# A triangular solver given to one engine and cut into parts, products tied to block sums, and separate load buffers for one engine's weights

## The chip, the core and the metric

The kernel runs on one core of a Trainium2 chip. Five engines work side by side, each through a fixed list of instructions: TensorE (PE, matrix products; PEld is its weight load), VectorE (DVE), ScalarE (ACT), GpSimd (POOL) and SyncE (SP), which issues nearly all transfers. An instruction waits until the results that it needs are there, and everything behind it on the same engine waits too. The metric is the time of one execution in device microseconds (us).

## The reference, cut to what matters

Two layers over 1024 tokens of width 1024, all in float32:

```python
h = rmsnorm(x, norm_w); proj = h @ w_in
attn = neighbourhood_attention(rmsnorm(aq), rmsnorm(ak), av, rpb) * silu(az)      # 8 heads of 64
# gated delta net, chunks of 64 tokens: a unit lower triangular system for each of 128 chunks
a_mat = where(strict, (kb @ k.T) * decay, 0) + eye(64)
sol = triangular_solve(a_mat, rhs, lower=True, unit_diagonal=True)
...
x1 = x + concat([attn, delta]) @ w_out
# second layer: rmsnorm, w_in_2 (8 heads of 128 with stick breaking, retention, merge logits), w_out_2
```

## The kernel before

**Matrix products.** A float32 operand is split into a high and a low part, and each product is made of three passes (hi·hi, hi·lo, lo·hi). The weights are loaded by rows of 128 (k = 0 to 7) into a tile called raw (L59 to 64, one SP transfer each) and split into wu. For most weights POOL makes both parts (L70 the high one, L71 the low one). With fast=True, used for w_out and for the eight heads of the second layer, the odd k go another way: ACT casts the high part (L67) and DVE subtracts (L68). All raw tiles come from one ring of three buffers, whoever splits them. dense_tok (L91) makes token tiles m of 128 in a PSUM bank of three ("acc").

**The solver.** X holds 128 systems, one per partition, of 64 rows by 64 columns, in SBUF. Column j from 62 down to 1 takes two instructions for each group of rows: multiply into a scratch tile (L457), add into X (L459). Rows from 8 up are DVE's (scratch svt, 512 elements), rows below 8 POOL's (scratch svq, 256), and the last eight columns DVE's. When all is done, X is stored to d_X, which the merges of the delta net read. The solver is a generator: take(sol, 4) emits four columns ahead of each of the 16 tiles of the neighbourhood attention na_attn, whose own work for a tile is two score products, a softmax (L554 to 557), transposes and the value products. take(prj, 1) emits a piece of the projection na_proj of the next pair of heads, with its normalisation of q and k (L490 to 500), beside it.

**The norm between the layers.** For half the tokens (s = 0) normalize(0) makes eight products (L911), each followed by a cast on ACT (h2h) and a subtraction (h2l, L913, even k on POOL, odd on DVE). They are emitted between the blocks of the other half of w_out, whose results residual() adds to the input (L860) and stores to d_x1. With s = 1 the same is done under the first head of the second layer.

**The order.** Nobody writes the engines' lists by hand: the code gives work in the order of its statements, and a scheduler with its own estimate of times makes a fixed list for every engine. So an edit in one place can move instructions of another.

## Time and profile before

| what | value |
|---|---|
| time, median of 3 executions | 2250.16 us (2249.15 to 2255.03) |
| time of the profiled execution | 2252.17 us |
| its span on the core | 2250.5 us |
| PE busy | 2163.0 us, 96% of the span |
| mean granted clock of PE | 0.984 |
| DVE, ACT, POOL busy | 1102.5, 766.0, 1105.4 us |

The span is what the profiler saw on the core; 1.67 us lie around it. PE is busy nearly all of the time, so time can be won only where PE stands still or runs at a lower clock. The stages with which the change has to do lie in the span as follows: the solver from 295 to 500 us, the norm between the layers from 786 to 840, the first head of the second layer from 837, the eight heads until 1370.

### The profile page before, as it was taken

The page shows a single profiled execution, that of the slowest core. Times are in us where ns is not written, and L with a number is a line of the kernel's source. Part 1 is how long each engine was busy: PE and PEld are TensorE (multiplying, and loading weights), DVE is VectorE, ACT ScalarE, POOL GpSimd, SP SyncE. Part 2 cuts the span into 40 slices and gives each one's busy share as a digit, 9 for nine tenths or more (in the row PEclk, how much of TensorE's full clock was granted, in tenths as well). Part 3 has the DMA queues.
Part 4 walks back from the last instruction along what each step waited for, and adds up shares of the span by engine and source line. Part 5 has one row for each costly group of instructions (what it writes and reads, how often), then busy time and mean ns, then how long its engine had stood idle before and what let it go on. Part 6 is the DMA issues. An engine that isn't in the chain of part 4 may idle for free.

```text
span 2250.5 us, 33410 instructions
## 1 busy us (share of the span) xinstructions
PE 2163.0 (96%) x12325; PEld 1882.8 (84%) x12325; DVE 1102.5 (49%) x1980; ACT 766.0 (34%) x1912; POOL 1105.4 (49%) x1451
## 2 busy tenths in 40 slices
PE   7999888899999999999999999999999999999999
PEld 7777777787889878999999998888988888878887
DVE  4688879953446553566555655123333432231321
ACT  5354433445555322444333433112222322321200
POOL 6667777773101345344333334356565755354532
PEclk9999999899999999999999999999999999999999
DMA  4255740126377542111111112212333323564433
GB/s 132 83 152 157 206 129 26 36 82 190 90 278 246 176 130 63 41 61 57 57 42 34 43 57 71 89 58 79 107 94 120 126 92 114 179 227 159 146 109 106
DMA packets 240196, 250.27 MB, mean 111 GB/s; under 512 B 40161, under 2 KB 175521, under 8 KB 239777
## 3 DMA queue, kind: packets, MB, share of 16 engines
q1 hardware_dynamic: 240032, 248.14, 35.3%
q8 instruction: 97, 1.59, 0.3%
q14 instruction: 67, 0.54, 0.1%
HBM read 172.56 MB, written 75.53 MB: 110 GB/s over the span
## 4 chain that ended last, share of the span: by engine, by line
PE 68%; DVE 11%; POOL 6%; issue 5%; DMA 5%; ACT 2%; SPq 1%; POOLq 0%; DVEq 0%; ACTq 0%
PE acc L112 29%; PE acc L102 17%; PE acc L853 3%; PE po L1083 2%; PE pz L1051 2%; DVE X L459 2%; DVE svt L457 2%; POOL wu L71 2%; DVE cv L314 1%; POOL wu L70 1%; DMA raw<-in_w_in_dram 1%; PE pz L546 1%; PE pt L563 1%; POOL ss L126 1%; PE pp L577 1%
## 5 line engine op out<-in xcount | busy, mean ns | idle before, releaser
L112 PE MATMUL acc<-h2h,wu 128*128 128x512 f32 x1440 | 438.4, 393 | 0.7 <-ACT lg L958 0.7
L102 PE MATMUL acc<-wu,h2h 128*128 128x384 f32 (+1 forms) x1536 | 366.8, 322 | 6.6 <-ACT lg L972 2.2
L71 POOL TENSOR_TENSOR wu<-raw,wu 128x512 fp32r<-128x512 f32 (+3 forms) x276 | 366.3, 1335 | 7.2
L70 POOL TENSOR_SCALAR wu<-raw 128x512 fp32r<-128x512 f32 (+3 forms) x276 | 205.8, 749 | 313.0 <-PE acc L112 202.4
L112 PEld LDWEIGHTS acc<-h2h,wu 128*128 128x128 f32 x1440 | 269.5, 188 | 54.9 <-ACT lg L958 1.1
L102 PEld LDWEIGHTS acc<-wu,h2h 128*128 128x128 f32 x1536 | 265.8, 191 | 11.6 <-ACT lg L972 2.6
L112 PE MATMUL acc<-h2l,wu 128*128 128x512 f32 x720 | 265.2, 392 | 0.0
L102 PE MATMUL acc<-wu,h2l 128*128 128x384 f32 (+1 forms) x768 | 244.9, 321 | 0.0
L102 PE MATMUL acc<-wu,h1hi 128*128 128x384 f32 (+2 forms) x768 | 192.2, 334 | 11.1 <-DVE kS L512 5.2
L112 PE MATMUL acc<-h1hi,wu 128*128 128x512 f32 x512 | 167.3, 416 | 6.8 <-ACT pad L309 3.2
L125 POOL TENSOR_SCALAR ss<-ss 128x2 f32<-128x2 f32 (+2 forms) x136 | 36.7, 270 | 269.6 <-ACT sq L1001 215.0
L112 PEld LDWEIGHTS acc<-h2l,wu 128*128 128x128 f32 x720 | 135.0, 188 | 26.5
L102 PEld LDWEIGHTS acc<-wu,h1hi 128*128 128x128 f32 x768 | 137.0, 195 | 16.0 <-issue 6.5
L102 PEld LDWEIGHTS acc<-wu,h2l 128*128 128x128 f32 x768 | 146.1, 191 | 1.6
L112 PEld LDWEIGHTS acc<-h1hi,wu 128*128 128x128 f32 x512 | 100.4, 198 | 31.8 <-ACT pad L309 4.2
L102 PE MATMUL acc<-wu,h1lo 128*128 128x384 f32 (+2 forms) x384 | 126.7, 333 | 0.0
L126 POOL TENSOR_TENSOR ss<-ss,mhalf 128x2 f32<-128x2 f32 (+2 forms) x136 | 118.9, 875 | 8.3
L112 PE MATMUL acc<-h1lo,wu 128*128 128x512 f32 x256 | 97.9, 411 | 0.0
L1001 ACT ACTIVATE sq<-acc 128x128 f32<-128x128 f32 x128 | 35.5, 286 | 138.7 <-PE acc L102 125.8
L314 DVE SCALAR_TENSOR_TENSOR cv<-pad,c_conv_w,cv 128x1024 f32<-128x1024 f32 x48 | 76.6, 1596 | 1.1
L112 PE MATMUL acc<-oah,wu 128*128 128x512 f32 x256 | 76.1, 393 | 1.0 <-DVE sg L1275 0.6
L102 PEld LDWEIGHTS acc<-wu,h1lo 128*128 128x128 f32 x384 | 74.8, 195 | 0.4 <-issue 0.2
(553 smaller groups left out, 4438.1 us busy)
## 6 DMA issues: line engine op xcount, KB each, us to landing
raw<-in_w_in_dram SPq DMA_DIRECT2D x192, 256.0 KB, 3.0
d_pk<-sct SPq DMA_DIRECT2D x24, 512.0 KB, 4.3
raw<-in_w_out_dram SPq DMA_DIRECT2D x40, 256.0 KB, 3.0
wsa<-d_pk SPq DMA_DIRECT2D x16, 512.0 KB, 6.4
wsb<-d_pk SPq DMA_DIRECT2D x16, 512.0 KB, 7.4
d_sg<-lg SPq DMA_DIRECT2D x32, 256.0 KB, 2.4
sg<-d_sg SPq DMA_DIRECT2D x32, 256.0 KB, 3.4
raw<-in_w_in_dram SPq DMA_DIRECT2D x32, 192.0 KB, 2.8
```

The source lines that it names most:

```text
L70: nc.gpsimd.tensor_scalar(out=u[:, 0, :], in0=raw, scalar1=1.0, scalar2=0.0, op0=ALU.mult, op1=ALU.add)
L71: nc.gpsimd.tensor_tensor(out=u[:, 1, :], in0=raw, in1=f32(u[:, 0, :]), op=ALU.subtract)
L102: nc.tensor.matmul(acc[:, :n], lhsT=hT[a][:, k, m * P:(m + 1) * P], rhs=us[k][:, b, c0:c0 + n], start=(k == 0 and i == 0), stop=(k == NK - ...
L112: nc.tensor.matmul(accs[half], lhsT=us[k][:, b, c0:c0 + P], rhs=hT[a][:, k, half * 512:(half + 1) * 512], start=(k == 0 and i == 0), stop= ...
L125: nc.gpsimd.tensor_scalar(out=dst, in0=src, scalar1=mul, scalar2=eps, op0=ALU.mult, op1=ALU.add)
L126: nc.gpsimd.tensor_tensor(out=dst, in0=dst, in1=mhalf[:, :eshape], op=ALU.pow)
L314: nc.vector.scalar_tensor_tensor(out=cv, in0=pad[:, i:i + T], scalar=conv_w[:, blk, i:i + 1], in1=cv, op0=ALU.mult, op1=ALU.add)
L457: eng.tensor_tensor(out=tv, in0=X[:, a:a + n, j:j + 1].to_broadcast([P, n, w]), in1=X[:, j:j + 1, j + 1:64].to_broadcast([P, n, w]), op=AL ...
L459: eng.tensor_tensor(out=X[:, a:a + n, j + 1:64], in0=X[:, a:a + n, j + 1:64], in1=tv, op=ALU.add)
L853: nc.tensor.matmul(acc, lhsT=us[k][:, y, (b % 4) * P:(b % 4 + 1) * P], rhs=token_set(mT[x][:, k, 0:T], s), start=(k == 0 and i == 0), stop ...
L1051: nc.tensor.matmul(pz[:, :w], lhsT=qk[0][a][:, i * P:(i + 1) * P], rhs=qk[1][b][:, c0:c0 + w], start=(x == 0), stop=(x == 2))
L1083: nc.tensor.matmul(po[:, i0 * P:512], lhsT=v[a][:, c0 // P + kb, :], rhs=wT[b][:, :n], start=(diag and kb == 0 and x == 0), stop=(diag == ...
```

## The change

It does five things. The solver has DVE alone, with one scratch tile of 512, is cut into 16 parts of about equal work, and each part is emitted behind a tile of na_attn instead of ahead of it. The products that normalise q and k read the PSUM bank themselves, where ACT copied q and k to SBUF first. The broadcast copy rb moves from DVE to ACT. Each product of the first norm (s = 0) is ordered behind the last residual sum emitted so far, and two are emitted after a block in place of one. And the raw tiles of odd k of the eight heads come from two buffers of their own (tag rawf), in the pool sr of the second layer.

```diff
-    def split_unit(src, ncol, pool=None, tag="wu", parts=1, fast=False, rpool=None):
-        raw = (rpool or wraw).tile([P, ncol], F32, tag="raw", name="raw", bufs=8 if rpool else 3)
+    def split_unit(src, ncol, pool=None, tag="wu", parts=1, fast=False, rpool=None, fpool=None):
+        if fast and fpool:
+            raw = fpool.tile([P, ncol], F32, tag="rawf", name="raw", bufs=2)
+        else:
+            raw = (rpool or wraw).tile([P, ncol], F32, tag="raw", name="raw", bufs=8 if rpool else 3)
...
-    def solver():
+    def solver(parts):
         tmp = svp.tile([P, 512], F32, name="svt")
-        tmq = svp.tile([P, 256], F32, name="svq")
-        LOW = 8
...
-        for j in range(62, 0, -1):
-            if j > LOW:
-                update(nc.vector, tmp, 512, LOW, j, j)
-            update(nc.gpsimd if j >= LOW else nc.vector, tmq, 256, 0, min(j, LOW), j)
-            yield 1
+            w = 63 - j
+            step = -(-j // -(-j * w // 512))
+            for a in range(0, j, step):
+                n = min(step, j - a)
+                tv = tmp[:, :n * w].rearrange("p (r c) -> p r c", r=n)
+                nc.vector.tensor_tensor(out=tv, in0=X[:, a:a + n, j:j + 1].to_broadcast([P, n, w]),
+                                        in1=X[:, j:j + 1, j + 1:64].to_broadcast([P, n, w]), op=ALU.mult)
+                nc.vector.tensor_tensor(out=X[:, a:a + n, j + 1:64], in0=X[:, a:a + n, j + 1:64], in1=tv, op=ALU.add)
+                did += n * w
+                if did * parts >= total * (at + 1):
+                    at += 1
+                    yield 1
...
-            nc.scalar.copy(out=qn[:, m, :], in_=acc[:, 0:128])
-            nc.scalar.copy(out=kn, in_=acc[:, 128:256])
             nc.scalar.copy(out=v[:, m, :], in_=acc[:, 256:384])
             for x, t_ in enumerate((qn[:, m, :], kn)):
-                t_ = t_.rearrange("p (h d) -> p h d", h=2)
-                nc.vector.tensor_tensor(out=t_, in0=t_, in1=ss[:, 2 * x:2 * x + 2].unsqueeze(2).to_broadcast([P, 2, 64]),
-                                        op=ALU.mult)
+                nc.vector.tensor_tensor(out=t_.rearrange("p (h d) -> p h d", h=2),
+                                        in0=acc[:, x * P:(x + 1) * P].rearrange("p (h d) -> p h d", h=2),
+                                        in1=ss[:, 2 * x:2 * x + 2].unsqueeze(2).to_broadcast([P, 2, 64]), op=ALU.mult)
...
-            nc.vector.tensor_copy(out=rb, in_=rs2.unsqueeze(2).to_broadcast([P, 2, 64]))
+            nc.scalar.copy(out=rb, in_=rs2.unsqueeze(2).to_broadcast([P, 2, 64]))
...
-    sol = solver()
-    take(sol, 2)
+    sol = solver(16)
...
-            take(sol, 4)
             take(prj, 1)
+            take(sol, 1)
...
+    turn = [None]
+
     def residual(pool, tag, bufs, acc, s, b):
...
-        nc.vector.tensor_tensor(out=xo, in0=acc, in1=xo, op=ALU.add)
+        turn[0] = nc.vector.tensor_tensor(out=xo, in0=acc, in1=xo, op=ALU.add)
...
-            nc.vector.scalar_tensor_tensor(out=xs[k], in0=xs[k], scalar=gain2[:, k:k + 1], in1=rs, op0=ALU.mult, op1=ALU.mult)
+            e = nc.vector.scalar_tensor_tensor(out=xs[k], in0=xs[k], scalar=gain2[:, k:k + 1], in1=rs, op0=ALU.mult, op1=ALU.mult)
+            if s == 0:
+                after(e, turn[0])
...
-            take(norm, 3 if b == 4 else 1)
+            take(norm, 3 if b == 4 else 2)
...
-            us = load_units(I["w_in_2"], 128 * h, 128, parts=4, stride=1024, fast=True)
+            us = load_units(I["w_in_2"], 128 * h, 128, parts=4, stride=1024, fast=True, fpool=sr)
```

How the lists of the engines move is shown at three places. A number at the head of a row is its place in the engine's list. L68, L860, L911 and L913 are L71, L863, L914 and L918 in the changed kernel; L1005 and L1007 keep their numbers.

The first place is DVE in the norm between the layers, from the first product of s = 0 on. Before:

```order
980 L911 SCALAR_TENSOR_TENSOR x_7789<-x_7789,c_norm_gain_7775,rs 128x512 [waits Activation_49]
981 L911 SCALAR_TENSOR_TENSOR x_7792<-x_7792,c_norm_gain_7775,rs 128x512 [waits DMAHW2_49]
982 L911 SCALAR_TENSOR_TENSOR x_7797<-x_7797,c_norm_gain_7775,rs 128x512 [waits DMAHW3_49]
983 L911 SCALAR_TENSOR_TENSOR x_7802<-x_7802,c_norm_gain_7775,rs 128x512 [waits DMAHW4_49]
984 L911 SCALAR_TENSOR_TENSOR xo<-xo,c_norm_gain_7775,rs 128x512 [waits DMAHW4_49]
985 L911 SCALAR_TENSOR_TENSOR xo<-xo,c_norm_gain_7775,rs 128x512 [waits DMAHW5_49]
986 L911 SCALAR_TENSOR_TENSOR xo<-xo,c_norm_gain_7775,rs 128x512 [waits DMAHW6_49]
987 L911 SCALAR_TENSOR_TENSOR xo<-xo,c_norm_gain_7775,rs 128x512 [waits DMAHW7_49,DVE_49]
988 L913 TENSOR_TENSOR h2l<-x_7792,h2h 128x512 [waits Activation_49]
989 L913 TENSOR_TENSOR h2l<-x_7802,h2h 128x512 [waits Activation_49]
990 L860 TENSOR_TENSOR xo<-acc,xo 128x512 [waits DMAHW1_49,PE_49,Pool_49]
```

And in the changed kernel:

```order
963 L914 SCALAR_TENSOR_TENSOR x_7588<-x_7588,c_norm_gain_7574,rs 128x512 [waits Activation_49]
964 L914 SCALAR_TENSOR_TENSOR x_7591<-x_7591,c_norm_gain_7574,rs 128x512 [waits DMAHW2_49]
965 L918 TENSOR_TENSOR h2l<-x_7591,h2h 128x512 [waits Activation_49]
966 L863 TENSOR_TENSOR xo<-acc,xo 128x512 [waits DMAHW1_49,PE_49,Pool_49]
967 L914 SCALAR_TENSOR_TENSOR x_7596<-x_7596,c_norm_gain_7574,rs 128x512 [waits DMAHW3_49]
968 L914 SCALAR_TENSOR_TENSOR x_7601<-x_7601,c_norm_gain_7574,rs 128x512 [waits DMAHW4_49]
969 L71 TENSOR_TENSOR wu<-raw,wu 128x512 [waits DMAHW2_49,Activation_49]
970 L863 TENSOR_TENSOR xo<-acc,xo 128x512 [waits DMAHW2_49,DVE_49]
971 L914 SCALAR_TENSOR_TENSOR xo<-xo,c_norm_gain_7574,rs 128x512 [waits DMAHW4_49]
```

Before, all eight products and two subtractions stand ahead of the residual sum L860; now two products and one subtraction stand ahead of it, and the other products follow in pairs behind later sums.

The second place is SP at the start of the first head. gqk are two small gain vectors, whose space is free only when the last products of w_out are done (the wait on PE), d_x_89 is the store of d_x1, and raw with 128x4x128 is a weight tile of a head. Before:

```order
393 L64 DMA raw<-in_w_in_dram 128x4x128 [waits DMAHW7_49,DMAHW2_49,DVE_49]
394 L861 DMA d_x_89<-xo 128x2x256 [waits DMAHW3_49,DVE_49]
395 L861 DMA d_x_89<-xo 128x2x256 [waits DVE_49]
396 L861 DMA d_x_89<-xo 128x2x256 [waits DMAHW5_49,DVE_49]
397 L64 DMA raw<-in_w_in_dram 128x4x128 [waits DMAHW0_49,Pool_49]
398 L64 DMA raw<-in_w_in_dram 128x4x128 [waits DMAHW1_49,DVE_49]
399 L64 DMA raw<-in_w_in_dram 128x4x128 [waits DMAHW2_49,Pool_49]
400 L984 DMA gqk<-in_sb_q_gain_dram 128x128 [waits PE_49]
401 L985 DMA gqk<-in_sb_k_gain_dram 128x128
402 L861 DMA d_x_89<-xo 128x2x256 [waits DMAHW3_49,DVE_49]
403 L64 DMA raw<-in_w_in_dram 128x256 [waits DMAHW6_49,DMAHW4_49,DVE_49]
```

And in the changed kernel:

```order
390 L67 DMA raw<-in_w_in_dram 128x4x128 [waits DMAHW2_49,Pool_49]
391 L862 DMA xo<-in_xT_dram 128x2x256 [waits DMAHW1_49,DVE_49]
392 L864 DMA d_x_89<-xo 128x2x256 [waits DVE_49]
393 L864 DMA d_x_89<-xo 128x2x256 [waits DMAHW3_49,DVE_49]
394 L864 DMA d_x_89<-xo 128x2x256 [waits DMAHW4_49,DVE_49]
395 L984 DMA gqk<-in_sb_q_gain_dram 128x128 [waits DMAHW5_49,PE_49]
396 L985 DMA gqk<-in_sb_k_gain_dram 128x128 [waits DMAHW6_49]
397 L864 DMA d_x_89<-xo 128x2x256 [waits DMAHW7_49,DMAHW1_49,DVE_49]
398 L67 DMA raw<-in_w_in_dram 128x4x128 [waits DMAHW0_49]
399 L67 DMA raw<-in_w_in_dram 128x4x128
400 L67 DMA raw<-in_w_in_dram 128x4x128 [waits DMAHW2_49,DMAHW0_49,DVE_49]
401 L67 DMA raw<-in_w_in_dram 128x4x128 [waits DMAHW3_49,DMAHW1_49,DVE_49]
```

Before, all eight weight tiles of the first head stand ahead of the gqk rows (397 to 399 are the last three); now the four of even k do (390 is the last), and the four of odd k stand behind gqk and behind the last store of d_x1, the third and the fourth of them (400 and 401) with a wait on DVE for their buffer.

The third place is DVE in the first head. L1005 and L1007 are the head's own work on a finished PSUM bank, which they release; L71 are the subtractions of odd weights, L914 and L918 the second norm (s = 1). Before:

```order
1014 L1005 TENSOR_TENSOR v<-acc,v 128x128 [waits PE_49,Activation_49]
1015 L900 COPY rt__8423<-pz 128x4 [waits PE_49]
1016 L1005 TENSOR_TENSOR v<-acc,v 128x128 [waits Activation_49]
1017 L1007 SCALAR_TENSOR_TENSOR sq<-acc,ss,gqk 128x128 [waits DVE_49,Pool_49]
1018 L1007 SCALAR_TENSOR_TENSOR sq<-acc,ss,gqk 128x128 [waits DMAHW2_49]
1019 L1007 SCALAR_TENSOR_TENSOR sq<-acc,ss,gqk 128x128 [waits Pool_49]
1020 L1007 SCALAR_TENSOR_TENSOR sq<-acc,ss,gqk 128x128
1021 L1005 TENSOR_TENSOR v<-acc,v 128x128 [waits PE_49,Activation_49]
1022 L68 TENSOR_TENSOR wu<-raw,wu 128x512 [waits DMAHW5_49,Activation_49]
1023 L1007 SCALAR_TENSOR_TENSOR sq<-acc,ss,gqk 128x128 [waits Pool_49]
1024 L1007 SCALAR_TENSOR_TENSOR sq<-acc,ss,gqk 128x128
1025 L911 SCALAR_TENSOR_TENSOR xo<-xo,c_norm_gain_7775,rs 128x512 [waits DMAHW3_49,Activation_49]
```

And in the changed kernel:

```order
995 L71 TENSOR_TENSOR wu<-raw,wu 128x512 [waits DMAHW1_49,Activation_49]
996 L71 TENSOR_TENSOR wu<-raw,wu 128x512 [waits DMAHW2_49,Activation_49]
997 L71 TENSOR_TENSOR wu<-raw,wu 128x512 [waits DMAHW3_49,Activation_49]
998 L914 SCALAR_TENSOR_TENSOR xo<-xo,c_norm_gain_7574,rs 128x512 [waits Activation_49]
999 L914 SCALAR_TENSOR_TENSOR xo<-xo,c_norm_gain_7574,rs 128x512
1000 L914 SCALAR_TENSOR_TENSOR xo<-xo,c_norm_gain_7574,rs 128x512 [waits DMAHW4_49]
1001 L914 SCALAR_TENSOR_TENSOR xo<-xo,c_norm_gain_7574,rs 128x512 [waits DMAHW7_49,DVE_49]
1002 L914 SCALAR_TENSOR_TENSOR xo<-xo,c_norm_gain_7574,rs 128x512 x4
1003 L918 TENSOR_TENSOR h2l<-xo,h2h 128x2x256 [waits Activation_49] x3
1004 L1005 TENSOR_TENSOR v<-acc,v 128x128 [waits PE_49,Activation_49] x2
1005 L918 TENSOR_TENSOR h2l<-xo,h2h 128x2x256 [waits Activation_49]
1006 L1007 SCALAR_TENSOR_TENSOR sq<-acc,ss,gqk 128x128 [waits Pool_49]
```

Before, the first four L1007 and more stand ahead of the second norm's products; now the subtractions of the four odd weights, all eight products and three of the second norm's subtractions stand ahead of the first L1005 and L1007.

## Rows read from the trace of the kernel before

**Rows 1.** The page's first part: busy time, share of the span, instructions.
```profile
PE 2163.0 (96%) x12325; PEld 1882.8 (84%) x12325; DVE 1102.5 (49%) x1980; ACT 766.0 (34%) x1912; POOL 1105.4 (49%) x1451
```
**Rows 2.** Windows: length, busy time of each engine (instructions), granted clock, DMA share.
```profile
300.00:460.00 160.00, 142.23 (x836) 119.36 (x835) 150.03 (x331) 64.15 (x176) 128.48 (x182) 0.93 0.14 44
460.00:500.00 40.00, 40.00 (x317) 34.64 (x316) 19.29 (x69) 18.84 (x44) 27.01 (x45) 1.00 0.22 61
```
**Rows 3.** The longest of PE's waits, 295 to 500 us: total, times, longest.
```profile
PE acc L102 <- DVE kS L512: 5.2, 2, 3.0
```
**Rows 4.** Windows view of X's instructions: length, DVE and POOL busy (instructions), clock.
```profile
295.00:500.00 205.00, 114.76 (x193) 93.10 (x156) 0.93 0.17 50
```
**Rows 5.** DVE by line, 295 to 500 us: busy, mean ns, idle before, releaser.
```profile
L500 DVE TENSOR_TENSOR qn<-qn,ss 128x128 f32<-128x128 f32 x17 | 8.4, 492 | 4.8 <-POOL ss L126 4.6
...
L587 DVE COPY rb<-rs 128x128 f32<-128x128 f32 x14 | 6.2, 440 | 0.1
...
L589 DVE TENSOR_TENSOR z<-po,z 128x128 f32<-128x128 f32 x7 | 2.0, 284 | 5.2 <-PE po L588 5.1
```
**Rows 6.** POOL by line in the same stretch.
```profile
L71 POOL TENSOR_TENSOR wu<-raw,wu 128x512 fp32r<-128x512 f32 (+1 forms) x24 | 29.7, 1239 | 0.0
```
**Rows 7.** DVE's timeline: single solver instructions (start, duration).
```profile
308.15 0.62 DVE L457 TENSOR_TENSOR svt<-X 128x450 f32<-128x450 f32 x1
...
499.60 0.22 DVE L457 TENSOR_TENSOR svq<-X 128x62 f32<-128x62 f32 x1
```
**Rows 8.** DVE's timeline in the first norm's stage.
```profile
798.97 3.79 DVE L911 SCALAR_TENSOR_TENSOR x<-x,c_norm_gain,rs 128x512 f32<-128x512 f32 x4 [7.51 <-ACT rs L907]
802.68 6.22 DVE L911 SCALAR_TENSOR_TENSOR xo<-xo,c_norm_gain,rs 128x512 f32<-128x512 f32 x4
...
811.54 0.68 DVE L860 TENSOR_TENSOR xo<-acc,xo 128x512 f32<-128x512 f32 x1
```
**Rows 9.** PE's waits from 800 to 912 us.
```profile
PE acc L853 <- DVE xo L860: 4.4, 1, 4.4
PE acc L102 <- ACT lg L972: 2.2, 1, 2.2
PE acc L102 <- DVE sq L1007: 1.6, 1, 1.6
```
**Rows 10.** Windows around the two stages after that, same columns.
```profile
812.30:833.00 20.70, 20.70 (x79) 16.73 (x80) 10.65 (x16) 5.52 (x10) 5.33 (x6) 0.88 0.63 203
833.00:837.00 4.00, 4.00 (x19) 3.24 (x18) 2.38 (x2) 0.60 (x1) 3.87 (x3) 1.00 0.42 128
837.00:850.20 13.20, 13.20 (x81) 13.19 (x79) 3.56 (x8) 3.24 (x13) 8.81 (x16) 1.00 0.48 141
905.90:912.00 6.10, 6.09 (x27) 6.09 (x28) 1.81 (x3) 0.92 (x2) 0.06 (x1) 0.72 0.43 132
```
**Rows 11.** SP's timeline: when transfers are issued, near 837 us.
```profile
837.71 0.50 SPq L984 DMA_DIRECT2D gqk<-in_sb_q_gain_dram  x1
...
838.78 0.38 SPq L861 DMA_DIRECT2D d_x<-xo  x1
```
**Rows 12.** The page's DMA issues: count, KB, median us from issue to landing.
```profile
raw<-in_w_in_dram SPq DMA_DIRECT2D x192, 256.0 KB, 3.0
```
**Rows 13.** DVE's timeline in the first head.
```profile
838.60 0.69 DVE L68 TENSOR_TENSOR wu<-raw,wu 128x512 fp32r<-128x512 f32 x1 [0.69 <-ACT wu L67]
...
859.69 8.54 DVE L911 SCALAR_TENSOR_TENSOR xo<-xo,c_norm_gain,rs 128x512 f32<-128x512 f32 x8
...
868.87 2.88 DVE L913 TENSOR_TENSOR h2l<-xo,h2h 128x512 fp32r<-128x512 f32 x4
```
**Rows 14.** ACT's timeline in the second head's loads.
```profile
904.65 0.62 ACT L67 CAST wu<-raw 128x512 fp32r<-128x512 f32 x1 [2.65 <-DMA raw<-in_w_in_dram]
905.17 0.68 ACT L972 ACTIVATE lg<-acc,bm 128x512 f32<-128x512 f32 x1
```
**Rows 15.** Windows view over the heads, columns as in rows 2.
```profile
918.50:1370.00 451.50, 447.47 (x2548) 414.40 (x2547) 265.02 (x516) 183.36 (x597) 175.59 (x372) 1.00 0.15 47
```

More of the change, by code (lines that the diff above doesn't have):

```diff
@@ L72, in split_unit, with load_units @@
         return u
-    def load_units(w, c0, width, parts=1, stride=0, pool=None, tag="wu", fast=False, rpool=None):
+    def load_units(w, c0, width, parts=1, stride=0, pool=None, tag="wu", fast=False, rpool=None, fpool=None):
         us = []
@@ L81, in load_units @@
                 src = rows[:, c0:c0 + parts * stride].rearrange("p (g s) -> p g s", g=parts)[:, :, :width]
-            us.append(split_unit(src, width * parts, pool, tag, parts, fast and k % 2 == 1, rpool))
+            us.append(split_unit(src, width * parts, pool, tag, parts, fast and k % 2 == 1, rpool, fpool))
         return us
@@ L444, in tile_kernel @@
     na = naB.__enter__()
-    def solver():
+    def solver(parts):
         tmp = svp.tile([P, 512], F32, name="svt")
-        tmq = svp.tile([P, 256], F32, name="svq")
-        LOW = 8
-        def update(eng, buf, size, r0, r1, j):
+        total = sum(j * (63 - j) for j in range(1, 63))
+        did, at = 0, 0
+        for j in range(62, 0, -1):
             w = 63 - j
-            step = -(-(r1 - r0) // -(-(r1 - r0) * w // size))
-            for a in range(r0, r1, step):
-                n = min(step, r1 - a)
-                tv = buf[:, :n * w].rearrange("p (r c) -> p r c", r=n)
-                eng.tensor_tensor(out=tv, in0=X[:, a:a + n, j:j + 1].to_broadcast([P, n, w]),
-                                  in1=X[:, j:j + 1, j + 1:64].to_broadcast([P, n, w]), op=ALU.mult)
-                eng.tensor_tensor(out=X[:, a:a + n, j + 1:64], in0=X[:, a:a + n, j + 1:64], in1=tv, op=ALU.add)
-        yield 1
-        for j in range(62, 0, -1):
-            if j > LOW:
-                update(nc.vector, tmp, 512, LOW, j, j)
-            update(nc.gpsimd if j >= LOW else nc.vector, tmq, 256, 0, min(j, LOW), j)
-            yield 1
+            step = -(-j // -(-j * w // 512))
[9 more added lines that the diff above has]
+                    yield 1
         nc.vector.memset(X.rearrange("p r c -> p (r c)")[:, 0:64 * 64:65], 1.0)
@@ L855, in out_blocks, with after @@
         return accs
+    NOSYNC = mybir.DependencyInfo(mybir.DependencyClass.NoSync, mybir.DependencyReason.DATA)
+    def after(later, earlier):
+        tc.add_manual_dep(later.ins, earlier.ins.name, NOSYNC, reason="engine order")
+    turn = [None]
     def residual(pool, tag, bufs, acc, s, b):
@@ L943, in tile_kernel @@
         return
-    NOSYNC = mybir.DependencyInfo(mybir.DependencyClass.NoSync, mybir.DependencyReason.DATA)
-    def after(later, earlier):
-        tc.add_manual_dep(later.ins, earlier.ins.name, NOSYNC, reason="table order")
     d_sg = dram.tile([16, P, T], F32, name="d_sg")
```

## The prediction

> **What bounds the kernel now.** I read the page's first part first. PE is busy 96% of the span [rows 1], so the whole of its idle time is 87 us and a change to other engines is worth only what it takes out of PE's gaps, and out of the stretches behind gaps in which PE has a lower granted clock. The windows view says where these are. From 300 to 460 us PE is busy 142.2 of 160 us at a granted clock of 0.93, while DVE is busy 150.0 of them [rows 2]. DVE is the bound of this stage, and PE's longest wait there is on it [rows 3]. From 460 to 500 us the picture turns round: DVE has 19.3 us of work in 40 and PE no gap at all. The solver takes 114.8 us of DVE and 93.1 us of POOL between 295 and 500 us [rows 4], so it is more than half of what loads DVE.
>
> Two other stages matter. Behind the norm between the layers PE waits 4.4 us once for the residual sum L860; near 905 us it waits 2.2 us for ACT's L972, and in the first head 1.6 us for DVE's L1007 [rows 9]. In the heads as a whole PE is busy 447.5 of 451.5 us at full clock [rows 15]: little is to be had there.
>
> **The solver, and the tiles' copies (A).** Cost of one instruction: 450 elements took 0.62 us and 62 took 0.22 us where nothing disturbed them [rows 7], so 1.03 ns an element and 0.156 us an instruction. DVE's share before is 192 instructions with 58,700 elements: 30.0 + 60.5 = 90.5 us, and it measured 114.8. After it is 212 instructions with 83,300 elements: 33.1 + 85.9 = 119.0 us. The disturbance of before, 24 us, comes while POOL reads SBUF too. POOL's solver work goes, its weight splitting stays: the subtractions alone are 29.7 us there [rows 6], the high parts come on top, in all about half of what the solver took. So I take a third to a half of the 24 us, and 130 us for the solver, 15 more than before.
>
> The Trainium skill ("SBUF — State Buffer", section "Who interferes with whom") says that a VectorE instruction with two SBUF inputs and a GpSimd instruction that reads SBUF shut each other out for a whole instruction, and that one with at most one SBUF input isn't touched. The trace agrees for the solver, 114.8 us where 90.5 were due. By that rule alone the 24 us shrink with POOL's reading time, and the solver would take some 127 us, 3 less than the sum goes by.
>
> Against the 15 us stand: rb leaves DVE, 14 copies and 6.2 us; the product on q takes 17 times 0.49 us with both inputs in SBUF, and a product of this size with a PSUM input takes 0.28 us [rows 5], so 3.5 us; and the tiles' other DVE work suffers less from POOL, a few us. DVE's load from 295 to 500 us stays what it was within some 5 us. What changes is its spread: equal parts to the end, in place of a list that is full until 460 us and half empty behind it, with each tile's own work emitted ahead of its part. 150 us of 160 plus 19.3 of 40 is 169 in 200; spread evenly, DVE is loaded to 85% where it was 94%. rb costs ACT about as much, and ACT gives up 64 copies of q and k; it is busy 64 of 160 us, which covers it. POOL only gains.
>
> PE's idle time of 300 to 460 us is 17.8 us. I take half of it, 8.9, since PE will still wait on DVE at some tiles, and 2 us of clock that comes back with it: **A = -11**. Bounds: 0, if the solver's instructions simply stand between the tile's in another way, and -18, if all the idle time goes and the clock stays as it is.
>
> **The first norm (B).** Before, eight products (3.79 + 6.22 us) and two subtractions stand ahead of the residual sum, which starts at 811.54 [rows 8]; PE waits 4.4 us for it. After, two products and one subtraction do: about 2 x 0.95 + 0.7 = 2.6 us from 798.97, so the sum is ready for its other inputs before 802. Its input tile comes later, when a buffer is free; it is late next, but the rows give it the 4.4 us that PE waited in any case. Then PE's clock: behind the gap 79 matmuls took 20.70 us at a clock of 0.88, and 19 took 4.00 us at 1.00 [rows 10]: 0.262 against 0.211 us, up to 4 us. Counted by whole matmuls at the edges it is less; I take 3. From 7.4 I take off 2 for new short waits, since later weights are now split among pairs of products: **B = -5.5**, bounds -7.5 and -2.
>
> **The first head (C).** Here the change costs something. T is 837.0, where the first head's matmuls begin; before, they run until 850.2 with no gap and at full clock [rows 10], because all eight weight tiles were loaded and split by then. After, the odd four stand in SP's list behind gqk, which is issued at T+0.7, and behind a store at T+1.8 [rows 11]. So k = 1 is issued at T+2.3, lands 3.0 us later [rows 12], is cast in 0.62 [rows 14] and subtracted in 0.69 us [rows 13]: ready at T+6.6. Two buffers serve four tiles: k = 5 is issued when k = 1 is subtracted, and is ready at T+11, k = 7 at T+11.8. PE does the three tiles m = 2, 3, 4 k by k; k = 0 is an eighth of 12.5 us, so it stands until T+6.6, and the other seven eighths, 10.9 us, end at T+17.5 in place of T+13.2: 4.3 us.
>
> Next: DVE's list has the four subtractions, the eight products of the second norm (8.54 us in one row [rows 13]) and three h2l subtractions (0.7 each) ahead of the first L1007, which frees the bank that PE wants for m = 5. They can't start before the last odd weight, T+11.8: 11.8 + 8.5 + 2.2 + about 2 for L1005 and L1007 = T+24.5. PE has run out of work at about T+18, so it waits some 6.5 us where it waited 1.6 [rows 9]: 5 more. With a clock that falls behind both gaps, about 2: **C = +11**. Bounds: +4, if only the first gap is real, and +14, if POOL's part of L1007's chain queues behind weights as well.
>
> **The second head's loads (E).** Before, ACT's casts wait for raw tiles, the last one 2.65 us, and L972 stands behind it [rows 14]; PE waits 2.2 us for L972, and then does 27 matmuls in 6.09 us at a clock of 0.72 [rows 10], where at 0.174 us each (12.5 us for 72 of them) they are 4.7. With buffers of their own the odd tiles are issued earlier and ACT comes past them: **E = -3.5**, bounds -3.6 and 0. In the later heads PE has no gaps that a weight tile makes, so the buffers are worth nothing there; the cover is PE's own work, and reordering there may bring a us either way.
>
> **Sum.** -11 - 5.5 + 11 - 3.5 = -9. The profiled execution is 2252.2 us, 2 us above the median of the runs, so 2243 for it and 2241 for the median.
>
> **Rivals.** (1) DVE stays the bound as it is: all parts of the solver are still ahead of something that PE wants, A is about 0, and the sum is +2, 2252: no change. For it: DVE's work doesn't shrink. Against it: the half-empty stretch behind 460 us. Undone raw buffers (E = 0) alone would give 2245, near the forecast. (2) The spread and the quieter POOL free PE from nearly all its waits: A = -18, the sum -16, 2234. For it: 85% of load leaves 30 us of air. Against: a late DVE answer costs PE time even with air elsewhere. (3) The solver overloads DVE. If POOL's weight splitting disturbs it as much as all of POOL did (a factor of 114.8 / 90.5 = 1.27), the solver takes 151 us, 36 more; DVE needs about 169 + 36 - 10 = 195 us of the 200 and cannot fill every gap between; taking its air of before in that load, 6% or 12 us, and some 8 us of waits for PE's answers, it runs some 15 to 20 us over 500 us, and the store of X and the merges behind it come as much later, with nothing in PE's list to fill it: -5.5 + 11 - 3.5 + 20 = +22, 2272 at worst. It decides from about 10 us over the end. (4) The first head costs more than all gains: with C at 14 and more of the second norm behind it (PE stands for the whole of a chain, +25), 2258. Its point is 18 us, where it outweighs A, B and E at half of A.
>
> By the rule above, rival (3) has the less to say for it, since only POOL's own reading time disturbs.
>
> **Chances.** What this kernel's measurement can tell from no change is 0.3%, 6.75 us: below 2243.4 is faster, above 2256.9 slower. Forecast 45%, rival 1 with unfulfilled gains 23%, rival 2 14%, rival 3 10%, rival 4 8%. Faster: a little more than two thirds of the forecast and all of rival 2, with a few per cent of neither: 48%. Same: the rest of the forecast and most of rival 1: 33%. Slower: rivals 3 and 4 and a remnant: 19%. The range leaves out about the upper half of rivals 3 and 4 and the far end of rival 2: 2229 to 2258. The forecast alone is 2234 to 2249.
>
> **What would show it.** A: in the windows from 300 to 460 us PE's busy time should rise from 142 to about 151, DVE's be about 85 to 90% in each of the windows up to 500, and X's rows on DVE sum to 125 to 135 us with none on POOL. B: no wait of PE on the residual sum near 808, and a clock near 1 from there to 837. C: from 837 on a wait of PE on ACT's or DVE's wu of about 4 us, and then one on L1007 of 6; SP's raw rows behind gqk. E: no wait on L972 near 905. The prediction is wrong if C doesn't appear (then about 2230), if the last X row is much later than 500 us, or if PE's waits between 300 and 460 keep their sum.

## The result

The changed kernel takes 2263.7 us (median of 5 executions, 2260.09 to 2266.92), the kernel before 2249.15 us in its 5; the ratio is 1.0069, with a 95% interval of 1.0052 to 1.0085. So it is slower, by some 15 us, and outside the predicted range of 2229 to 2258. The profiled execution took 2260.09 us with a span of 2258.4 and was the fastest of its five; that of before took 2252.17, 3.0 us more than the median of its five. So the two traces are 7.9 us apart where the medians are 14.6.

The page's first part and, below it, the windows view of the solver's stage and of the first head in the trace of after, with the columns of [rows 1] and [rows 2]:

```profile
PE 2157.2 (96%) x12325; PEld 1879.6 (83%) x12325; DVE 1109.8 (49%) x1968; ACT 765.0 (34%) x1882; POOL 1025.7 (45%) x1295
```

```profile
300.00:460.00 160.00, 145.84 (x873) 123.83 (x872) 145.60 (x320) 64.27 (x158) 60.63 (x64) 0.95 0.12 37
460.00:500.00 40.00, 39.44 (x302) 33.72 (x301) 36.61 (x87) 17.77 (x43) 12.68 (x16) 1.00 0.21 57
836.00:849.00 13.00, 11.60 (x63) 11.51 (x63) 8.41 (x10) 5.45 (x9) 12.14 (x13) 0.87 0.49 144
849.00:862.00 13.00, 2.25 (x13) 1.93 (x12) 8.41 (x10) 3.74 (x14) 12.67 (x14) 0.71 0.14 40
862.00:866.00 4.00, 2.96 (x9) 2.99 (x10) 2.43 (x6) 1.30 (x6) 3.83 (x9) 0.50 0.24 66
866.00:880.00 14.00, 14.00 (x62) 12.07 (x62) 1.51 (x5) 1.37 (x6) 3.94 (x6) 0.93 0.31 95
```

From 300 to 460 us PE is busy 145.8 us, 3.6 more than before, and from 460 to 500 us DVE is busy 36.6 of 40 us, where it was 19.3. The last solver instruction ends at 499.5 us (500.1 before), so the solver doesn't run over. But the attention doesn't end sooner: its last score product starts at 716.2 us, before at 714.0. What PE wins in the stage it has lost just ahead of it. From 250 to 300 us, before and then after:

```profile
250.00:300.00 50.00, 41.31 (x217) 37.28 (x217) 31.26 (x58) 16.11 (x53) 31.54 (x40) 0.92 0.70 173
250.00:300.00 50.00, 32.63 (x179) 30.33 (x180) 27.79 (x57) 14.03 (x38) 24.74 (x28) 0.84 0.74 189
```

PE's two longest waits from 240 to 310 us are now 7.0 us for kt (the normalised keys of the delta net, 3.3 us before) and 6.4 us for qd (a copy of q with which an attention tile begins; none before). The first attention tile stands earlier in PE's list: its first score product starts at 297.7 us, before at 312.9. And from 849 to 862 us PE is nearly empty. The three longest of PE's waits from 560 to 920 us (total, times, longest):

```profile
PE acc L105 <- DVE sq L1007: 11.8, 1, 11.8
PE pz L901 <- DVE qa L896: 2.2, 1, 2.2
PE acc L105 <- ACT wu L70: 1.4, 1, 1.4
```

The wait of 4.4 us on the residual sum and that of 2.2 us on L972 [rows 9] are gone. In their place PE waits 11.8 us for L1007. Marks along PE's list show where the time went. The first head starts at 831.4 us (837.0 before) though the attention ended 2 us later, so the norm between the layers won some 8 us here. The first score product of a head starts at 920.4 us (911.8 before), so the first head and the loads beside it lost 14.2.

The odd weight tiles are late as forecast. From SP's and ACT's timelines (start, duration):

```profile
831.60 0.35 SPq L984 DMA_DIRECT2D gqk<-in_sb_q_gain_dram  x1
...
832.53 0.38 SPq L864 DMA_DIRECT2D d_x<-xo  x1
832.96 24.26 SPq L67 DMA_DIRECT2D raw<-in_w_in_dram  x13
...
837.14 1.29 ACT L70 CAST wu<-raw 128x512 fp32r<-128x512 f32 x2 [4.12 <-DMA raw<-in_w_in_dram]
```

They stand behind gqk and the store of d_x1, and ACT's first two casts wait 4.1 us for them. PE waits 1.4 us for such a tile (wu) itself. The 2.2 us are for qa, the sums of squares of the second norm, which PE's list now takes up at 835 us, behind the first weight tiles; before, it took them up at 845 us without a wait.

Why L1007 is late stands in three engines' timelines (start, duration). ACT has squared the first bank at 851.3 us. DVE then waits 4.88 us for ss, the factors of the head's norm, so it had finished what stands ahead of L1007 at 857.4. POOL takes up the first of the two instructions for the first ss at 858.6 and the second at 861.6, with weight splits and subtractions before and between:

```profile
850.98 0.27 ACT L1001 ACTIVATE sq<-acc 128x128 f32<-128x128 f32 x1
...
843.68 8.99 DVE L914 SCALAR_TENSOR_TENSOR xo<-xo,c_norm_gain,rs 128x512 f32<-128x512 f32 x8
...
862.29 0.61 DVE L1007 SCALAR_TENSOR_TENSOR sq<-acc,ss,gqk 128x128 f32<-128x128 f32 x2 [4.88 <-POOL ss L129]
...
855.71 1.15 POOL L74 TENSOR_TENSOR wu<-raw,wu 128x256 fp32r<-128x256 f32 x1
856.83 1.71 POOL L918 TENSOR_TENSOR h2l<-xo,h2h 128x512 fp32r<-128x512 f32 x1
858.62 0.19 POOL L128 TENSOR_SCALAR ss<-ss 128x2 f32<-128x2 f32 x1
858.89 0.41 POOL L73 TENSOR_SCALAR wu<-raw 128x256 fp32r<-128x256 f32 x1
859.26 0.72 POOL L74 TENSOR_TENSOR wu<-raw,wu 128x256 fp32r<-128x256 f32 x1
859.94 1.26 POOL L918 TENSOR_TENSOR h2l<-xo,h2h 128x512 fp32r<-128x512 f32 x1
...
861.56 0.70 POOL L129 TENSOR_TENSOR ss<-ss,mhalf 128x2 f32<-128x2 f32 x1
```

POOL is busy 12.7 of the 13 us from 849 to 862, so its list is full there. But it stood still ahead of that. The second norm's factors rt, which come from the same sums qa, now stand in POOL's list ahead of the splits, and POOL waits 14.1 us for them; before, it took them up without a wait, behind the first two ss. After and before:

```profile
836.70 0.20 POOL L128 TENSOR_SCALAR rt__8222<-rt__8222 128x4 f32<-128x4 f32 x1 [14.09 <-DVE rt__8222 L903]
...
850.31 0.20 POOL L125 TENSOR_SCALAR rt__8423<-rt__8423 128x4 f32<-128x4 f32 x1
```

The kernel with the buffers alone (e2, below) shows the same order with a wait of 17.9 us. No run changes only this order, so its share of the 11.8 us is open.

### The profile page after: what moved, and what is told of

Read it like the earlier page. It is cut to its first block, busy times and chain, and to the rows that moved or that the text cites. A ratio compares the mean times of both kernels' runs of the same rounds, so it can differ in the third digit from the quotient of the medians.

```text
span 2258.4 us, 33159 instructions
## 1 busy us (share of the span) xinstructions
PE 2157.2 (96%) x12325; PEld 1879.6 (83%) x12325; DVE 1109.8 (49%) x1968; ACT 765.0 (34%) x1882; POOL 1025.7 (45%) x1295
## 4 chain that ended last, share of the span: by engine, by line
PE 73%; DVE 9%; POOL 5%; issue 5%; DMA 4%; ACT 2%; SPq 1%; POOLq 0%; ACTq 0%; DVEq 0%
PE acc L115 30%; PE acc L105 19%; PE acc L849 3%; PE po L1083 2%; PE pz L1051 2%; DVE cv L317 2%; POOL wu L74 2%; DVE X L461 1%; DVE svt L459 1%; POOL wu L73 1%; PE pz L543 1%; PE acc L969 1%; PE pt L560 1%; PE pt L1204 1%; PE pp L574 1%
## 5 line engine op out<-in xcount | busy, mean ns | idle before, releaser
L105 PE MATMUL acc<-wu,h2h 128*128 128x384 f32 (+1 forms) x1536 | 368.6, 323 | 16.1 <-DVE sq L1007 11.8
L74 POOL TENSOR_TENSOR wu<-raw,wu 128x512 fp32r<-128x512 f32 (+3 forms) x276 | 370.7, 1353 | 7.6
L73 POOL TENSOR_SCALAR wu<-raw 128x512 fp32r<-128x512 f32 (+3 forms) x276 | 210.9, 768 | 319.1 <-PE acc L115 227.1
L128 POOL TENSOR_SCALAR ss<-ss 128x2 f32<-128x2 f32 (+2 forms) x136 | 36.2, 266 | 378.2 <-ACT sq L1001 241.4
L115 PE MATMUL acc<-h1hi,wu 128*128 128x512 f32 x512 | 162.7, 406 | 7.2 <-ACT pad L312 4.1
L129 POOL TENSOR_TENSOR ss<-ss,mhalf 128x2 f32<-128x2 f32 (+2 forms) x136 | 119.8, 881 | 9.2
```

Source lines behind the costliest of these rows:

```text
L73: nc.gpsimd.tensor_scalar(out=u[:, 0, :], in0=raw, scalar1=1.0, scalar2=0.0, op0=ALU.mult, op1=ALU.add)
L74: nc.gpsimd.tensor_tensor(out=u[:, 1, :], in0=raw, in1=f32(u[:, 0, :]), op=ALU.subtract)
L105: nc.tensor.matmul(acc[:, :n], lhsT=hT[a][:, k, m * P:(m + 1) * P], rhs=us[k][:, b, c0:c0 + n], start=(k == 0 and i == 0), stop=(k == NK - ...
L115: nc.tensor.matmul(accs[half], lhsT=us[k][:, b, c0:c0 + P], rhs=hT[a][:, k, half * 512:(half + 1) * 512], start=(k == 0 and i == 0), stop= ...
L128: nc.gpsimd.tensor_scalar(out=dst, in0=src, scalar1=mul, scalar2=eps, op0=ALU.mult, op1=ALU.add)
L129: nc.gpsimd.tensor_tensor(out=dst, in0=dst, in1=mhalf[:, :eshape], op=ALU.pow)
```

## The experiments

Each ratio is to the kernel before, from runs on the same chip. Where microseconds stand beside a ratio without being medians, they are the ratio times 2249.

**One edit taken out of the change: no separate buffers (e1).** Edit:

```diff
-  us = load_units(..., fast=True, fpool=sr)
+  us = load_units(..., fast=True)
```

> The changed kernel with one edit undone: the heads' odd weight tiles come from the shared ring of three again. Theory R (the separate buffers lose the time in the first head): the wait of 11.8 us on L1007 near 851 and the 3.6 us on qa and wu before it go, with their slow clock; from the start of the first head to its scores it takes 75 us as before the change, not 89. Time about 6 us under the kernel before, 2243, ratio 0.997. Theory S (the solver on one engine loses it, spread over many places): the time stays 8 us or more above the kernel before, ratio 1.004 or more.

Measured: 2250.49 us, ratio 1.0008 (0.9995 to 1.0021). The 11.8 us wait was gone, and from the start of the first head on the list is as before. PE waits 1.5 us for L1007 and 1.7 us for L972 again. So the buffers are most of the loss; but 2243 didn't come, so something else loses some 7 us.

**The buffers alone on the kernel before (e2).** Edit: `fpool=sr` and its two helpers, nothing else.

> The kernel before with only the separate buffers for odd weight tiles. Theory R: the first head stretches by 14 us (PE waits near 12 us on L1007 behind POOL's queue, and some 4 us on the odd tiles), the rest is as before: 2263, ratio 1.006. Theory S: within 3 us of the kernel before, since the odd tiles are hidden elsewhere.

Measured: 2264.63 us, ratio 1.0074 (1.0057 to 1.0091), 17 us. The waits of the first head are those of after, in a kernel that has nothing else of the change:

```profile
PE acc L105 <- DVE sq L1010: 11.5, 1, 11.5
PE pz L901 <- DVE qa L896: 2.2, 1, 2.2
PE acc L105 <- ACT wu L70: 0.6, 1, 0.6
```

**The ordered first norm alone (e3).** Edit: `turn[0]`, `after(e, turn[0])` for s = 0, and two products taken after a block.

> The kernel before with only the first norm's products ordered two by two behind the residual sums. Theory R: no wait on the residual sum near 808 and full clock behind it, the first head begins 6 us sooner and nothing takes it back: 2243, ratio 0.997. Rival: the 6 us are given back in the first head, since its weights and the second norm are late by as much: ratio 1.000.

Measured: 2243.86 us, ratio 0.9977 (0.9965 to 0.9989), 5 us won. The wait on the residual sum is gone and the clock from 812 to 833 us is 1.00 (0.88 before), a new wait of 1.7 us on a weight (wu, L71) stands there, and nothing is given back in the first head.

**Solver, products from PSUM and rb together (e4).** Edit: the changed solver, na_proj and rb on the kernel before.

> The kernel before with only the solver on DVE in 16 parts, the products on q and k from PSUM, and rb on ACT. Theory R: nothing won and 0 to 3 us lost, because PE's waits only change their places: ratio 1.000 to 1.0015. Theory S: 8 us or more lost, ratio 1.004 or more. My prediction's term for it was 11 us won, ratio 0.995.

Measured: 2255.17 us, ratio 1.0031 (1.0018 to 1.0045): 7 us lost where I had 11 won. My prediction's term has the wrong sign.

**The solver alone (e5).** Edit: the changed solver and where it is taken; ACT's copies of q and k and DVE's rb as before.

> The kernel before with the solver alone moved to DVE in 16 parts behind the tiles; q and k are still copied by ACT and rb is still made by DVE. The three parts together lost 7.5 us. Theory O (the order of the lists near 250 to 300 us is what loses: an early attention tile put ahead of projection work, on which PE waits 6 to 7 us twice): here it depends on whether the solver's new place makes that order; if so the loss is 5 to 8 us, ratio 1.002 to 1.0035. Theory L (DVE's added load loses it): ratio 1.004 or more here, since DVE keeps rb and the products from SBUF, and PE's waits on DVE between 310 and 500 us grow.

Measured: 2244.02 us, ratio 0.9976 (0.996 to 0.9991): 5.4 us won, with 2.0 to 9.0 in the interval. The early tile isn't in this kernel's list (the first score product starts at 311.0 us), which agrees with theory O but doesn't test it; theory L falls, since DVE has the whole solver here and the time goes down. Windows of this kernel:

```profile
300.00:460.00 160.00, 151.86 (x900) 127.26 (x899) 149.35 (x341) 70.25 (x186) 64.59 (x70) 0.95 0.16 48
460.00:500.00 40.00, 39.55 (x347) 35.29 (x346) 36.56 (x91) 17.54 (x44) 17.00 (x17) 1.00 0.30 93
```

PE is busy 151.9 of 160 us, 9.6 more than before and what I had forecast for this window (about 151).

**Products from PSUM and rb without the solver (e6).** Edit: the other two parts of e4.

> The kernel before with only the products on q and k from PSUM and rb on ACT; the solver stays on two engines. Theory O: if these edits make the early order, the loss is here, ratio 1.002 to 1.003, with the waits of PE near 255 and 290 us. Theory L: DVE is relieved by some 10 us in its fullest stretch, and the time falls by 2 to 6 us, ratio 0.998.

Measured: 2255.77 us, ratio 1.0035 (1.0019 to 1.005). Theory L falls again, since DVE is relieved here and the time goes up. The waits of theory O stand in this list (7.0 us for kt, 5.0 us for qd); what they are worth isn't shown yet.

**The products from PSUM alone (e9).** Edit:

```diff
-  nc.scalar.copy(out=qn[:, m, :], in_=acc[:, 0:128])
-  nc.scalar.copy(out=kn, in_=acc[:, 128:256])
...
-  in0=t_
+  in0=acc[:, x * P:(x + 1) * P]
```

> The kernel before with only the products on q and k reading the PSUM bank, without ACT's copies. Theory P (these products keep the bank until POOL's row sums are there, PE's projection waits for it, and the lists are made with the first attention tile ahead of projection work): PE's waits of 7 us on kt near 255 us and of 5 to 6 us on qd near 290 us stand here too, and the loss is 5 to 8 us, ratio 1.002 to 1.0035. Rival (rb on ACT loses it): ratio 0.999 to 1.001.

Measured: 2259.85 us, ratio 1.0047 (1.0035 to 1.006): 10.6 us lost, more than the 5 to 8 that I expected. In the traces PE stands idle 18.3 us from 246 to 310 us (13.0 before), 21.5 from 310 to 520 us (14.7 before) and 5.3 from there to 725 us (7.4 before). The two longest of PE's waits from 240 to 310 us:

```profile
PE po L349 <- DVE kt L340: 7.0, 1, 7.0
PE po L529 <- ACT qd L526: 5.2, 1, 5.2
```

ACT's, POOL's and DVE's work on one bank of this kernel, in the timeline:

```profile
346.53 0.39 ACT L490 ACTIVATE sq<-acc 128x256 f32<-128x256 f32 x1 [1.95 <-PE acc L102]
...
346.81 0.26 ACT L495 COPY v<-acc 128x128 f32<-128x128 f32 x1
...
347.81 0.46 POOL L125 TENSOR_SCALAR ss<-ss 128x4 f32<-128x4 f32 x1 [0.87 <-DVE mx L554]
...
348.35 1.30 POOL L126 TENSOR_TENSOR ss<-ss,mhalf 128x4 f32<-128x4 f32 x1
...
350.37 0.28 DVE L497 TENSOR_TENSOR qn<-acc,ss 128x128 f32<-128x128 f32 x1
...
350.57 0.28 DVE L497 TENSOR_TENSOR kn<-acc,ss 128x128 f32<-128x128 f32 x1
```

The copy of v is the last reader of the bank by ACT and ends at 347.07 us. The products on q and k need POOL's row sums and end at 350.85, 3.8 us later. Before, the copies of q and k stand ahead of that of v, and the bank is free with it, 0.9 us after the first read:

```profile
346.48 0.38 ACT L490 ACTIVATE sq<-acc 128x256 f32<-128x256 f32 x1
...
347.06 0.30 ACT L497 COPY v<-acc 128x128 f32<-128x128 f32 x1
```

Over the 32 token tiles of e9 the products end 0.5 to 12.2 us behind the copy of v, 5.3 in the mean. From the first read to the last a bank is held 6.0 us in the median, before 0.9. The first three tiles, which take all three banks, are among the longest: their copies of v end at 250.5 to 252.5 us, their products between 260.6 and 264.7. In the kernel before, PE goes on with the projection at 251.65 us. In e9 its list has, from 249.7 to 264.1 us, the transposes that wait for kt and no projection. The first line is of before, the others of e9:

```profile
251.65 0.62 PE L102 MATMUL acc<-wu,h1hi 128*128 128x384 f32 x2 [1.12 <-ACT v L497]
...
259.09 1.12 PE L349 MATMUL po<-ident,kt 128*128 128x128 f32 x4 [7.01 <-DVE kt L340]
...
264.14 0.60 PE L102 MATMUL acc<-wu,h1hi 128*128 128x384 f32 x2
```

PE's waits that end with such a product and hold a projection product up directly come to only 4.0 us from 310 to 520 us. The rest of the loss shows as waits on other things, in lists that came out another way. That the longer hold made them so is likely, and not shown by itself.

**rb on ACT alone (e10).** Edit: `nc.vector.tensor_copy` of rb becomes `nc.scalar.copy`.

> The kernel before with only the broadcast copy rb on ACT. Theory P: DVE is 6 us lighter from 295 to 500 us and ACT has room: 0 to 3 us won, ratio 0.9985 to 1.000. Rival: ACT makes rb late behind its casts and the value products wait: 3 to 8 us lost, ratio 1.0015 to 1.0035.

Measured: 2254.5 us, ratio 1.0021 (1.001 to 1.0033): 4.7 us lost. ACT's row for rb, by line from 295 to 500 us:

```profile
L587 ACT COPY rb<-rs 128x128 f32<-128x128 f32 x14 | 4.2, 298 | 10.6 <-DVE z L594 5.2 <-DVE rs L585 2.8 <-PE po L588 2.4
```

And the first of PE's waits from 310 to 520 us:

```profile
PE pt L563 <- ACT s L557: 6.0, 3, 2.6
```

ACT stands idle 10.6 us ahead of its 14 copies, because they wait for DVE or PE, and PE waits 6.0 us for the exponential s L557, before 1.6 in all. But the one doesn't lead to the other. The last copy of rb stands 5 to 15 us ahead of the three exponentials, and two of these, behind PE's waits of 2.2 and 2.6 us, waited themselves, for DVE's maximum mx:

```profile
383.69 0.72 ACT L557 ACTIVATE s<-s,mx 128x512 f32<-128x512 f32 x1 [4.20 <-DVE mx L556]
...
453.06 0.72 ACT L557 ACTIVATE s<-s,mx 128x512 f32<-128x512 f32 x1 [7.58 <-DVE mx L556]
```

Ahead of the later one DVE does solver instructions up to 451 us. So the copy's place on ACT costs 4.7 us, with a list of DVE that came out another way beside it, and how it costs them isn't shown.

**First tile put back (e14).** Edit to e9: the first attention tile's transposes ordered behind the last z product of na_proj.

```diff
-  nc.tensor.transpose(po[...], qd[...], ident)
+  tr = nc.tensor.transpose(po[...], qd[...], ident)
+  if p == 0 and t == 0:
+      after(tr, col_end[0])
```

> The products on q and k from PSUM alone, with the first attention tile's transposes ordered behind the last of the z products on PE, as they stand in the kernel before. Theory D (the early first tile in PE's list is what loses: PE stands 5 us for qd): the wait on qd near 290 us goes, and the loss of 10 us shrinks to 4 or less, ratio below 1.002. Theory B (the bank held until the row sums are there loses it, at every token tile of the projections): the waits only move, ratio 1.0035 to 1.005.

Measured: 2256.83 us, ratio 1.0034 (1.0024 to 1.0044). The wait on qd near 290 us went, and waits on kn came in its place:

```profile
PE acc L513 <- DVE kn L504: 9.5, 2, 7.1
PE po L356 <- DVE kt L347: 7.0, 1, 7.0
```

The waits moved, as theory B says, and the whole interval lies above the 1.002 of theory D, so the early tile isn't all of the loss. By the ratios it is 3 of the 10.6 us; by the two intervals it can be anything from nothing to somewhat over half. The longest waits here are of the transposes L513, which need kn itself and also a bank that such a product frees; the view doesn't tell which of the two came last.

**ACT makes the products itself (e15).** Edit: four scaled copies on ACT from the bank in place of two plain ones and DVE's two products.

> The kernel before with ACT making the products on q and k itself from the PSUM bank (four scaled copies in place of two plain ones and DVE's two products). The bank is held as long as with the products on DVE from PSUM, and DVE is lighter by 13 us. Theory B: it loses about as much, ratio 1.003 to 1.005. Theory D: the early tile stands in this list too, so it loses by that alone, with PE's wait near 290 us. If DVE's place in the chain is what loses, it is at 1.001 or below.

Measured: 2259.16 us, ratio 1.0043 (1.0027 to 1.0059). DVE has nothing to do with q and k here, and the loss is the same. This list has the early tile too, so it speaks for theory B against DVE's place in the chain, not against D. And ACT itself now waits for the row sums, 41.0 us in 17 waits from 240 to 520 us, with all of its list behind; the run doesn't separate that from the bank.

**Buffers from the second head on (e7).** Edit: `fpool=sr if h else None` and the ordered norm, on the kernel before.

> The kernel before with the ordered first norm, and the separate buffers for odd weight tiles from the second head on only; the first head takes the shared ring. Theory G (the loss of the separate buffers is the place of the first head's odd tiles behind the gain vectors in SP's list, and what follows from it): no wait of 11 us, the first head as before, and the wait on L972 near 905 gone: 1 to 3 us less than with the norm alone, ratio 0.996 to 0.9975. Rival: the buffers lose in every head: ratio 1.002 or more.

Measured: 2241.13 us, ratio 0.997 (0.9956 to 0.9983). PE doesn't wait for L972, and 0.7 us for L1007. So what the buffers lose comes from the first head. Beyond it, the five later heads whose score products can be compared take 64.7 us each in the trace, 64.5 or 64.6 with the norm alone (e3).

**No early merge weights (e8).** Edit to e2: the line `take(early, 1 + (n_ == 3))` of the first head taken out, so that this work is done under the second.

> The kernel before with the separate buffers, but the early merge products and their eight weight tiles are emitted under the second head instead of the first. Theory Q (of PE's 11.5 us wait on L1007, some 5 come from weight tiles that POOL splits ahead of the row sums ss): the wait falls to 6 to 8 us and the time by 3 to 6 us against the separate buffers alone, ratio 1.005. Rival: the wait is set by DVE's eight products of the second norm alone: it stays at 10 us or more, ratio 1.007.

Measured: 2268.13 us, ratio 1.0089 (1.0069 to 1.0109). PE's waits from 829 to 960 us:

```profile
PE acc L105 <- DVE sq L1010: 8.7, 1, 8.7
PE acc L1030 <- DVE sq L1010: 2.2, 2, 1.8
```

The wait on L1007 (here L1010) falls from 11.5 to 8.7 us, and 2.2 us come back at another product. In the trace the first head is 19.0 us shorter than in e2, with the moved products out of it, and the next two heads together are 22.0 us longer; the difference in time to e2 is within the noise. So the early weight tiles are at most 3 us of the wait and, with what comes back, less than 1. In this list POOL takes up the first ss at 862.4 us right behind four subtractions of the second norm, which follow DVE's products. The forecast was a miss, in time and in the wait.

**Without the losing parts (e11, e12, e13).** Edits to the kernel before: e11 has the solver, the ordered norm, and the buffers from the second head on; e12 has rb on ACT besides; e13 is e11 without the buffers.

> What is left of the change when the losing parts are out: the solver on DVE in 16 parts, the ordered first norm, and the separate buffers from the second head on; q and k are copied by ACT, rb is made by DVE. If the parts add up: 5 us from the solver and 7 from norm and buffers: 2237, ratio 0.9947. If they share one gain, such as the same clock: 0.997.

> As the kernel without the losing parts, with rb on ACT: the changed kernel with two edits undone, the products from PSUM and the first head's separate buffers. If these two are all that loses, the time is 26 us under the changed kernel's 2264, at 2236 to 2240, ratio 0.994 to 0.996; if rb on ACT loses too, it is 3 us or more above the same kernel with rb on DVE.

> The solver on DVE and the ordered first norm alone, on top of the kernel before: the kernel without the losing parts, and without the separate buffers. If the buffers from the second head on are worth what the wait on L972 and the slow clock behind it cost (2 to 3.5 us), this one is that much slower, 2240, ratio 0.9955; if they are worth nothing, it is at 2237, ratio 0.994.

Measured: e11 2237.25 us, ratio 0.9942 (0.9928 to 0.9956); e12 2240.9 us, 0.9958 (0.9944 to 0.9971); e13 2239.49 us, 0.9962 (0.9948 to 0.9977). e11 beats both kernels: 13 us under the kernel before, some 26 under the changed one. By the medians rb on DVE is 3.7 us better than on ACT, and the buffers are worth 2 us (4.5 by the ratios); in both pairs the intervals overlap, so neither is clear of the noise. In the traces the stretch from the first head's start to its first score product is 4.8 us shorter with the buffers (70.3 us in e11, 75.1 in e13).

## Why the prediction was wrong

The edits each by itself, as ratios times 2249: buffers +17, products from PSUM +11, rb +5, solver -5, norm -5. Unrounded they add up to +21 and the change measured +15; products and rb together cost 8 and not 15, so these two share their loss, and with the solver they cost 7. The parts don't simply add.

**A, the solver's stage: forecast -11, measured +7. The failed step is the one that took the products from PSUM and rb for savings.** The prediction counted what they save on DVE and wrote that ACT's copies fall away. It didn't ask what those copies did for PE: they freed the PSUM bank before the row sums were there. I priced the edit at DVE's 3.5 us and put the bank at nothing. By itself the edit costs 10.6 us (e9), and the bank is held 6.0 us in the median instead of 0.9. That the longer hold loses the time is what the lists and waits of e9 suggest; no run gives the projection another bank, and the early first tile's share stays open. For rb the step was "ACT is busy 64 of 160 us, which covers it". ACT had the time, and the edit still costs 4.7 us (e10); by which path stays open. DVE's load from 295 to 500 us, which was to stay within 5 us, rose from 173.9 to 185.4 us.

The solver by itself was rightly seen: PE's busy time from 300 to 460 us rose as forecast (e5), and the time fell, by 5.4 us where half of PE's idle time made 8.9, which the interval of e5 just includes. In the changed kernel its DVE time was 140.0 us, not 130:

```profile
290.00:500.00 210.00, 140.01 (x213) 0.95 0.16 50
```

Rival 1 (nothing won here) had DVE's order for its reason. Rival 3 (the solver overloads DVE) is out, since the solver ends at 499.5 us and e5 gains. No rival had the bank.

**B, the first norm: forecast -5.5, measured -5 (e3).** Right by its own steps: the 4.4 us and the slow clock went, and a new wait of 1.7 us came on a weight, for which I had taken off 2.

**C, the first head: forecast +11, with +14 as its bound; the buffers alone measured +17 with E's gain in it. The mechanism was right, and the second of its two terms was mis-sized.** The gaps at the start of the head are the 2.2 and 1.4 us of waits shown above, where I had 4.3. The wait on L1007 was to be 6.5 us and was 11.8. I let L1007 follow DVE's list (products, subtractions, L1005); that list was done at 857.4 us. But its factor ss is made on POOL, and POOL's list has splits of the early merge weights and subtractions of the second norm ahead and between: the two instructions for the first ss started at 858.6 and 861.6 and ended at 862.3. DVE's 4.9 us of waiting for it are nearly all of the 5.3 us that the term is short. I had POOL only as a bound, and not its 14.1 us of standing still beforehand. The clock in the windows behind the wait is 0.50 (1.2 GHz) from 862 to 866 us and 0.93 to 880, some 3 us by these windows, where I allowed 2. Rival 4 had this size of C, at 8%, but no loss in A.

**E, the second head's loads: forecast -3.5.** The wait on L972 is gone in after, e7 and e11; the medians of e13 and e11 make it -2, those of e3 and e7 -3, neither clear of the noise.

So the sum of -9 failed by A's wrong sign, 18 us, and by the size of C, some 9 us (C and E together were to be +7.5 and were +17). That is 27 us where some 24 are to be explained, since the parts don't simply add.

## What to carry to other kernels

When a copy is removed, ask what it released, not only what it cost: an early copy out of PSUM frees the bank, and an instruction that reads the bank at the end of a chain keeps it for the whole chain (in the median 6.0 us here instead of 0.9). An engine with free time is not a free place: ACT was busy 64 of 160 us, and a copy of 0.3 us a time moved to it still cost 4.7 us. And before buffers are given a pool of their own, look what stands ahead of the loads in the queue, and how the lists of all engines change: the same buffers lost 17 us in the first head and won perhaps 2 or 3 behind it.

## What the runs showed of the hardware

The solver's DVE instructions took 21 us over what their sizes make (140.0 less 119.0) though POOL does no solver work any more; while POOL did, they took 24 over. Set against POOL's timeline instruction by instruction, with the size's time of 1.03 ns an element and 156 ns each taken off, 20.5 of the 21 us fall on the 41 solver instructions that overlap POOL's weight splits (L73 and L74), and 0.1 us on the 39 that overlap only POOL's row sums and powers on 128x4 (L128 and L129). Before, the 39 that overlap splits lost 14.5 us and the 74 that overlap only POOL's solver work lost 7.6. Two of the rows that lost most after the change, from DVE's timeline:

```profile
319.81 1.45 DVE L461 TENSOR_TENSOR X<-X,svt 128x300 f32<-128x300 f32 x1
...
322.12 1.47 DVE L461 TENSOR_TENSOR X<-X,svt 128x325 f32<-128x325 f32 x1
```

300 elements should take 0.47 us. So POOL's solver work is gone, and with it up to 10 of the 24 us (94 instructions overlapped it and no split), but the splits now take 6 us more: 41 instructions lose 0.50 us each, where 39 lost 0.37. The Trainium skill ("SBUF — State Buffer", section "Who interferes with whom") has a VectorE instruction with two SBUF inputs contend with a GpSimd instruction that reads SBUF, for a pair of ports that is locked exclusively. The trace agrees for the splits, which take 0.74 us (L73) and 1.31 us (L74) in the mean. It doesn't for POOL's powers: L129 on 128x4 takes 1.13 us in the mean, and the 18 solver instructions that overlap it alone lost 0.04 us in all. So the time that a POOL instruction takes in the profile isn't what counts; those that disturb here are those on 128x256 and 128x512 elements. And the shrinking in proportion to POOL's time that I had forecast, to a third or a half of the 24 us, came out at 21.
